# A hybrid decoder layer on one core: evacuations ordered behind dense products, inverses from blocks of 16, relayout transfers issued by SP

## The chip, the cores and the metric

The kernel runs on one core of a Trainium2 chip. The metric is the device time of one execution in microseconds (us). Engines: PE (TensorE) multiplies, DVE (VectorE), ACT (ScalarE) and POOL (GpSimd) work elementwise, SP (SyncE) issues most transfers; 16 DMA engines move data.

## The reference

The input is x of 1024 tokens x 1024 features, all float32, one layer:

```python
def swiglu(h, w1, w3, w2):
    return (jax.nn.silu(h @ w1) * (h @ w3)) @ w2
x = x + 0.5 * swiglu(rmsnorm(x, ffn1_norm), ...)          # D_FF = 2816
p = rmsnorm(x, mix_norm) @ w_in
y = concat(rwkv7_mixer(p[:D_SHIFT]), gmlp_mixer(pu, pv))  # 512 + 512 wide
x = x + y @ w_out
x = x + 0.5 * swiglu(rmsnorm(x, ffn2_norm), ...)
x = rmsnorm(x, final_norm)
```

The block above is condensed. The RWKV-7 mixer (8 heads of 64) is a recurrence over tokens, with a normalised key `kk = k*k_k / |k*k_k|`:

```python
sa = S @ a_t                      # a_t = -kk
S  = S * decay_t + sa b_t^T + v_t k_t^T   # b_t = kk * a
y_t = S @ r_t
```

The gMLP mixer multiplies by a causal 128 x 128 matrix inside chunks of 128 tokens.

## The kernel before, in words

**Dense products.** Every dense product is made of three products of 128x512 tiles in a reduced float32 format: each operand is split into a high part (ACT, a cast) and a low part (what the cast lost, a subtraction on DVE or POOL), and high x high, high x low and low x high are added up (`HI_LO`). `mm` (L192, instruction at L193) issues such a product, `rmm` (L201) a small one of the recurrence. The operands `wsp` (weights), `xt`, `xc` (activations) come from these splits.

**Stages.** FFN1 (to about 700 us), mixer (to about 1490), FFN2. Each FFN uses seven products p = 1..7 of half-size operands in place of eight. `down` (L478) runs p in the order 1, 5, 2, 3, 6, 7, 4; each p has 11 steps of 12 dense products. A step's `operands` (L483) loads weights and the hidden rows, forms differences on DVE (L493 to L497), casts on ACT (L500, L501) and makes low parts on DVE (L502) and POOL (L503). A finished bank is added to the residual by `add` (L519, instruction L521) on DVE: 12 additions after p = 1 and after p = 6, 8 after p = 7, 4 after each other one. `add` is given a high priority at the end and a place between products otherwise. In the last stage the final norm of row half 0 scales eight tiles (L716).

**Mixer.** w_in's columns come as weight pieces by `w_cols`, with the low part on POOL or DVE (L743). `pair` (L942) prepares decay, keys and values for two heads; it needs 1/|k|^2 per token and head, which `spread2` (L925, products `hm,sq`) and `back2` (L933, products `con,i`) sum and spread back. The recurrence runs in eight "octs" of 128 tokens (class `Oct`), each in chunks of 64. `prep` (L1120) forms SC, the products of keys with keys inside a chunk; `invert` (L1169) inverts 8x8 diagonal blocks on DVE, for which SC is written to DRAM (`ldr`, L1143), read back as blocks (`M`, L1172), the inverse written (`tdr`, L1187) and read back as `T` (L1191), all issued by ACT; `merge` (L1194) doubles the block size in three levels (8, 16, 32), each with products T,SC, then T,X and X,T; `chain` (L1226) carries the state S; `finish` (L1264) normalises the output (products `con,Y`). `w_out` (L766) multiplies by the output projection in two column halves, 192 products for each half of the tokens. `first_half` (L331) is FFN2's up product for one half of the tokens; it calls a `hook` into which the second `w_out` and then its statistics (products `one,xs`, `con,rr_r`) and `build`/`x_build` (`xc` tiles for the other half) are put.

**What sets the order.** The program is a set of Python tasks with a clock of their own (`Flow`): a task that says `yield 4.0` is resumed when 4.0 us of emitted work have passed, so these numbers set where its instructions stand among the others. A list scheduler then orders instructions by priority (`PR_RWKV`, `PR_CHAIN`, `PR_EVAC`) and by dependences. Each engine runs its instructions in that order.

Of the kernel before, what the change touches and what calls it, by code (L numbers as in the profile page):

```python
# [16 lines left out]
P = 128  # L17
# [28 lines left out]
CON = [("ident", 128), ("me", 128), ("m8", 32), ("m16", 32), ("m32", 32), ("bo", 128), ("cm", 256), ("tri", 128)]  # L46
# [7 lines left out]
def host_constants():  # L54
# [10 lines left out]
        **{f"m{b}": (s64 // (2 * b) == t32 // b) & (s64 // b % 2 == 1) for b in (8, 16, 32)},  # L65
# [82 lines left out]
class K:  # L148
    def __init__(self, ctx, tc, a, out):
# [12 lines left out]
        self.edge = None  # L162
# [28 lines left out]

    def mm(self, *args, **kw):  # L192
        i = self.nc.tensor.matmul(*args, **kw)  # L193
        if self.edge is not None:
# [75 lines left out]
    def apply(self, dst, res, gain, rb, out=None, ks=range(KT)):  # L270

        nc = self.nc
        for k in ks:
            t = self.xtp.tile([P, HALF], F32, name="silu", bufs=3)
            nc.vector.scalar_tensor_tensor(t, res[k // 2][:, k % 2], self.v(gain, k), rb, op0=ALU.mult, op1=ALU.mult)
# [202 lines left out]
    def down(self, pool, w2, res, done, loads):  # L478
# [40 lines left out]
        def add(p, bank, row, k):  # L519
            rv = res[row][k // 2][:, k % 2]  # L520
            ve.scalar_tensor_tensor(rv, bank, 0.5, rv, op0=ALU.mult, op1=ALU.add)  # L521
            done(p, row, k)

        for p, y, new, outs in plan:
# [18 lines left out]
            for o in outs:  # L543
                for f in range(4):
# [42 lines left out]
    def program(self):  # L587
# [39 lines left out]
        def task(row):  # L627
            yield 1.0
            rb = yield from self.spread(accs[row], "d" if row == 0 else "e", 2.5)
            if row == 0:  # L630
                rb = self.keep(rb)
                xm[0] = self.halves()
                for k in range(KT):
                    self.apply(xm[0], res[0], "gm", rb, ks=[k])
# [34 lines left out]
        yield ("rwkv", 0)  # L669
        accs = ([], [])  # L670
        out0 = yield from self.w_out(0, xres, accs[0], (self.mp, "h", 3))
# [6 lines left out]
        def hook(s):  # L678
            if state["done"] or not (("rwkv", 1) in flow.done or s >= 12):
# [4 lines left out]
        def second():  # L684
            yield ("rwkv", 1)
            crp.close()
            cm.close()
            p1, c1 = self.open("p1")
            yield from self.w_out(1, xres, accs[1], (p1,))
# [5 lines left out]
            rb1 = yield from self.spread(accs[1], "e")  # L695
            c1.close()
            cxq.close()
            flow.spawn(self.build(xres[1], "g2", w2, rbs2, stats2, ("xb", 1), True))
# [8 lines left out]
        def out(row):  # L707
# [5 lines left out]
            for k in range(KT):  # L713
                with self.hp(0 if row == 0 else PR_EVAC):
                    rv = res[row][k // 2][:, k % 2]
                    nc.vector.scalar_tensor_tensor(rv, rv, self.v("gf", k), rb, op0=ALU.mult, op1=ALU.mult)  # L716
# [35 lines left out]
    def w_cols(self, w, j, eng=None):  # L752
        return self.wtile([KT, P], w[j].rearrange("p (k n) -> p k n", k=KT), eng)
# [12 lines left out]
    def w_out(self, half, xres, acc, sums):  # L766
# [3 lines left out]
        for hf in range(2):  # L770
# [5 lines left out]
            for n, k in enumerate([4, 5, 6, 7, 0, 1, 2, 3]):  # L776
                raw = self.ws.tile([P, 2, HALF], F32, name="raw", bufs=RAWB)
# [19 lines left out]
    def mixer_consts(self):  # L797
# [20 lines left out]
        self.hm = mp.tile([P, 2], F32, name="hm")  # L818
        nc.scalar.copy(self.hm, self.c["bo"][:, 0::64])
        self.X = [mp.tile([P, NB, CH], F32, name=f"X{i}") for i in range(3)]  # L820
# [9 lines left out]
        nc.gpsimd.memset(self.S, 0.0)  # L830
        self.pcc = [mp.tile([P, PR, HALF // CH], F32, name=f"pcc{h}") for h in range(2)]
# [93 lines left out]
    def spread2(self, src):  # L925

        ps = self.psum("e")
        for t in range(4):
            self.rmm(ps[:, 2 * t:2 * t + 2], lhsT=src[:, t * P:(t + 1) * P], rhs=self.hm,
                     start=(t == 0), stop=True, skip_group_check=True)  # L930
        return ps[:, 0:8]

    def back2(self, small):  # L933
        ps = self.psum("e")
        for t in range(4):
            for h in range(2):
                self.rmm(ps[HS[h], t * P:(t + 1) * P],
                         lhsT=small[:, 2 * t + h:2 * t + h + 1].broadcast_to([P, CH]), rhs=self.c["ident"],
# [402 lines left out]
```

## Time and profile before

| | us |
|---|---|
| median of 3 runs | 2114.07 |
| lowest, highest | 2109.13, 2115.06 |
| profiled execution, its own time | 2114.52 |
| its span | 2112.4 |
| PE busy in it | 1971.0 (93%) |
| DVE, ACT, POOL busy | 1160.4 (55%), 700.5 (33%), 975.3 (46%) |
| mean granted PE clock | 0.962 of full |

Shares of busy time are means over stages. A matmul record of 128x512 in the timeline stands with its count (x132); in brackets stands the idle time of the engine before the group and what ended it. PEclk is the granted TensorE clock as a share of the full one (2.4 GHz; the lower level is 1.2 GHz).

### The profile page before, as it was taken

Reading aid. Unit: us, or ns where it says so; the run is one execution under the profiler, and the core shown is the slowest. Engines: PE = TensorE matmul, PEld = TensorE weight load, DVE = VectorE, ACT = ScalarE, POOL = GpSimd, SP = SyncE. Lnnn points to the kernel's source line nnn. Section 1 sums busy time; section 2 is a strip of 40 time slices with the busy share of each in tenths; the row PEclk is TensorE's granted clock in tenths of the full one; section 3 lists DMA queues with packets and bytes.
Section 4 is the critical chain, followed back from the end, with each engine's and each line's share of the span. In section 5 each row is a group of like instructions: output and inputs, shape, how many; then the busy total and the mean of one; then the engine's idle time right before and its main releaser. Section 6 shows DMA issues by size and latency. Waiting matters only on the chain. (4 is left out here: it accounts for less than half of the span.)

```text
span 2112.4 us, 34477 instructions
## 1 busy us (share of the span) xinstructions
PE 1971.0 (93%) x13408; PEld 1613.1 (76%) x13408; DVE 1160.4 (55%) x1645; ACT 700.5 (33%) x1205; POOL 975.3 (46%) x749
## 2 busy tenths in 40 slices
PE   6999999998998999999899898997899999999987
PEld 5787888887876778767788777876678888878866
DVE  6716666646658354445534344324756666655576
ACT  5433222223443443241312122233442222224432
POOL 3426665554555565353323133124455666545542
PEclk9999999999999999999999998998899999999998
DMA  8655444447644576553443455435654544476452
GB/s 284 237 165 170 169 159 160 159 149 275 195 151 139 194 242 212 130 203 106 149 132 98 118 157 177 118 126 188 212 175 162 170 168 159 136 264 193 141 178 101
DMA packets 235187, 360.34 MB, mean 171 GB/s; under 512 B 68240, under 2 KB 101008, under 8 KB 235024
## 3 DMA queue, kind: packets, MB, share of 16 engines
q1 hardware_dynamic: 181248, 342.43, 49.0%
q10 hardware_dynamic: 53776, 15.71, 3.2%
q8 instruction: 105, 1.72, 0.3%
q14 instruction: 58, 0.48, 0.1%
HBM read 260.53 MB, written 97.53 MB: 170 GB/s over the span
## 5 line engine op out<-in xcount | busy, mean ns | idle before, releaser
L193 PE MATMUL psd<-xt,wsp 128*128 128x512 f32 x1920 | 490.0, 412 | 12.4 <-ACT silu L352 3.9
L193 PEld LDWEIGHTS psd<-xt,wsp 128*128 128x128 f32 x1920 | 369.3, 196 | 107.2 <-DVE wsp L743 4.9
L743 POOL TENSOR_TENSOR wsp<-raw,wsp 128x512 fp32r<-128x512 f32 x170 | 228.9, 1367 | 363.2 <-ACT wsp L740 353.3
L193 PE MATMUL psd<-xc,wup 128*128 128x512 f32 x1584 | 374.8, 389 | 4.0 <-ACT wup L257 3.6
L193 PE MATMUL psd<-wsp 128*128 128x512 f32 x1440 | 342.6, 397 | 14.1 <-ACT wsp L501 9.5
L193 PEld LDWEIGHTS psd<-xc,wup 128*128 128x128 f32 x1584 | 297.0, 188 | 67.2 <-ACT wup L257 4.5
L193 PEld LDWEIGHTS psd<-wsp 128*128 128x128 f32 x1440 | 271.9, 191 | 77.1 <-ACT wsp L501 11.4
L503 POOL TENSOR_TENSOR wsp<-raw,wsp 128x512 fp32r<-128x512 f32 x154 | 230.1, 1498 | 215.6 <-ACT wsp L501 165.7
L193 PE MATMUL pse<-xc,wup 128*128 128x512 f32 x1056 | 254.4, 389 | 0.0
L258 POOL TENSOR_TENSOR wup<-wraw,wup 128x512 fp32r<-128x512 f32 x132 | 179.0, 1365 | 127.2 <-ACT wup L257 126.2
L193 PEld LDWEIGHTS pse<-xc,wup 128*128 128x128 f32 x1056 | 198.0, 188 | 41.5 <-ACT wup L257 0.5
L740 ACT CAST wsp<-raw 128x512 fp32r<-128x512 f32 x246 | 139.7, 617 | 150.1 <-PE psd L193 98.5
L502 DVE TENSOR_TENSOR wsp<-raw,wsp 128x512 fp32r<-128x512 f32 x110 | 104.9, 966 | 80.1 <-ACT wsp L500 79.9
L385 DVE TENSOR_TENSOR wt<-wraw 128x512 f32<-128x512 f32 x44 | 42.1, 958 | 183.1 <-DMA wraw<-in_ffn_w_dram 183.1
L257 ACT CAST wup<-wraw 128x512 fp32r<-128x512 f32 x132 | 81.3, 619 | 179.4 <-PE psd L193 109.7
L193 PE MATMUL pse<-wsp 128*128 128x512 f32 x396 | 110.1, 406 | 17.2 <-DVE wsp L502 12.7
L500 ACT CAST wsp<-raw 128x512 fp32r<-128x512 f32 x110 | 68.2, 620 | 165.8 <-PE psd L193 65.3
L193 PE MATMUL psc<-wsp 128*128 128x512 f32 x396 | 106.8, 399 | 0.0
L501 ACT CAST wsp<-raw 128x512 fp32r<-128x512 f32 x154 | 94.9, 617 | 32.4 <-DMA raw<-hd 25.7
L193 PEld LDWEIGHTS pse<-wsp 128*128 128x128 f32 x396 | 76.7, 196 | 36.7 <-DVE wsp L502 15.9
L743 DVE TENSOR_TENSOR wsp<-raw,wsp 128x512 fp32r<-128x512 f32 x76 | 60.4, 828 | 69.2 <-ACT wsp L740 56.5
L193 PEld LDWEIGHTS psc<-wsp 128*128 128x128 f32 x396 | 76.5, 194 | 16.4
(225 smaller groups left out, 2509.0 us busy)
## 6 DMA issues: line engine op xcount, KB each, us to landing
wraw<-in_ffn_w_dram SPq DMA_DIRECT2D x88, 512.0 KB, 4.6
raw<-hd SPq DMA_DIRECT2D x154, 256.0 KB, 3.5
raw<-in_ffn_w_dram SPq DMA_DIRECT2D x132, 256.0 KB, 3.2
raw<-in_ffn_w_dram SPq DMA_DIRECT2D x44, 512.0 KB, 4.3
raw<-in_w_in_dram SPq DMA_DIRECT2D x36, 512.0 KB, 4.1
hd<-u SPq DMA_DIRECT2D x66, 256.0 KB, 2.5
hd<-s SPq DMA_DIRECT2D x66, 256.0 KB, 5.0
sd<-silu SPq DMA_DIRECT2D x44, 256.0 KB, 3.4
```

The costliest lines, as they stand in the source:

```text
L193: i = self.nc.tensor.matmul(*args, **kw)
L257: nc.scalar.copy(t[:, 0], src)
L258: eng.tensor_tensor(t[:, 1], src, t[:, 0].bitcast(F32), op=ALU.subtract)
L385: ve.tensor_sub(t1, b12, b11)
L500: nc.scalar.copy(t[:, 0, 0], w)
L501: nc.scalar.copy(t[:, 0, 1], h)
L502: ve.tensor_tensor(t[:, 1, 0], w, t[:, 0, 0].bitcast(F32), op=ALU.subtract)
L503: ge.tensor_tensor(t[:, 1, 1], h, t[:, 0, 1].bitcast(F32), op=ALU.subtract)
L740: self.nc.scalar.copy(dst[:, 0, sl], src[:, sl])
L743: eng.tensor_tensor(dst[:, 1, sl], src[:, sl], dst[:, 0, sl].bitcast(F32), op=ALU.subtract)
```

## The change

Six parts. (1) `pace`: an order dependence without a semaphore that puts an instruction behind the last dense product emitted so far; used for `add` (except p = 4), the mixer's first activations and the final scalings of row half 0. The list of late additions goes f by f. (2) The inverse is made of 16x16 blocks on 64 partitions: two 8x8 inverses at a time and then the off-diagonal block by two multiplications and two reductions; `merge` has two levels. The waits of `invert` are 7.0, one 2.0 and 9.0. (3) ldr, M, tdr and T are issued by SP. (4) `spread2` and `back2` are gone: 16 one-column products per pair sum the squares, and 1/|k|^2 scales SC (four DVE operations of 128x128 per tile) and Bt (DVE in place of an ACT copy). (5) Low parts of `w_cols` alternate between DVE and POOL. (6) `w_out` waits for the recurrence only before its fifth of eight pieces; the hook for the second half waits for the last chain or s = 17; statistics and `build` behind it are a task of their own.

```diff
+    def pace(self, i):
+        self.tc.add_manual_dep(i.ins, self.last.name,
+                               mybir.DependencyInfo(mybir.DependencyClass.NoSync, mybir.DependencyReason.DATA),
+                               reason="order")
...
-            ve.scalar_tensor_tensor(rv, bank, 0.5, rv, op0=ALU.mult, op1=ALU.add)
+            i = ve.scalar_tensor_tensor(rv, bank, 0.5, rv, op0=ALU.mult, op1=ALU.add)
+            if p != 4:
+                self.pace(i)
...
-            for o in outs:
-                for f in range(4):
+            for f in range(4):
+                for o in outs:
...
-            if state["done"] or not (("rwkv", 1) in flow.done or s >= 12):
+            if state["done"] or not (("chain", 2 * NO - 1) in flow.done or s >= 17):
...
     def w_cols(self, w, j, eng=None):
+        if eng is None:
+            self.turns = 1 - self.turns
+            eng = self.nc.vector if self.turns else self.nc.gpsimd
...
             for n, k in enumerate([4, 5, 6, 7, 0, 1, 2, 3]):
+                if hf == 0 and n == 4:
+                    yield ("rwkv", half)
+                    sums = ready()
...
-        ss = self.spread2(sq)
+        ss = self.psum("e")
+        for i in range(HALF // CH):
+            for s in HS:
+                self.rmm(ss[s, i:i + 1], lhsT=sq[s, i * CH:(i + 1) * CH], rhs=self.one[s], start=(i == 0), stop=True,
+                         skip_group_check=True)
...
-        inv = self.back2(i8)
-        ve.tensor_mul(a, a, inv)
...
+                        nc.vector.scalar_tensor_tensor(d[:, p], m[:, p], inv[:, p, k:k + 1], c["me"],
+                                                       op0=ALU.mult, op1=ALU.mult)
...
-        nc.scalar.dma_start(M, self.diag(self.ldr))
+        nc.sync.dma_start(M, self.diag(self.ldr))
...
-        yield 4.0
+        yield 7.0
...
-            if t % 2:
-                yield 0.6
+            if t == 5:
+                yield 2.0
...
-                nc.scalar.dma_start(self.T[HS[h], n], self.matT(td[n], h))
-        yield 6.0
+                nc.sync.dma_start(self.T[HS[h], n], self.matT(td[n], h))
+        yield 9.0
...
-        for lvl, bs in enumerate((8, 16, 32)):
+        for lvl, bs in enumerate((16, 32)):
```

DVE at the change from p = 1 to p = 5 in FFN1's down product, before. L493 forms differences, L502 low parts, L521 the additions (`rd` and `res` are the residual's tiles, `psd` the banks):

```order
L493 TENSOR_TENSOR dt<-raw,dt 128x512
L502 TENSOR_TENSOR wsp<-dt,wsp 128x512
L521 SCALAR_TENSOR_TENSOR rd<-psd,rd 128x512 x4
L521 SCALAR_TENSOR_TENSOR res<-psd,res 128x512 x8
L493 TENSOR_TENSOR dt<-raw,dt 128x512 x4
L502 TENSOR_TENSOR wsp<-dt,wsp 128x512 x2
```

The same place of the changed program, where L504, L513 and L532 are the lines of the same three operations:

```order
L504 TENSOR_TENSOR dt<-raw,dt 128x512 x2
L513 TENSOR_TENSOR wsp<-dt,wsp 128x512
L532 SCALAR_TENSOR_TENSOR rd<-psd,rd 128x512
L532 SCALAR_TENSOR_TENSOR res<-psd,res 128x512 x2
L532 SCALAR_TENSOR_TENSOR rd<-psd,rd 128x512
L504 TENSOR_TENSOR dt<-raw,dt 128x512
L513 TENSOR_TENSOR wsp<-dt,wsp 128x512
L504 TENSOR_TENSOR dt<-raw,dt 128x512 x2
L532 SCALAR_TENSOR_TENSOR res<-psd,res 128x512 x2
```

The twelve additions stood in one block and now stand a few at a time among differences and low parts.

PE at the end of the recurrence and the second `w_out` (the 192 products `psd<-wsp`), before; `psd<-xt,wsp` are dense products of FFN2's first half, `psd<-xc,wup` the first that need x_build's tiles:

```order
L202 MATMUL psc<-WA,Bt 64x64 x8
L193 MATMUL psd<-xt,wsp 128x512 x12
L202 MATMUL psc<-WA,SC 64x64 x8
L202 MATMUL pse<-con,Y 64x64 x16
L193 MATMUL psd<-wsp 128x512 x192
L202 MATMUL pse<-one,xs 128x1 x8
L202 MATMUL pse<-con,rr_r 128x128 x4
L193 MATMUL psd<-xt,wsp 128x512 x216
L193 MATMUL psd<-xc,wup 128x512 x2
```

And now:

```order
L210 MATMUL psc<-WA,SC 64x64 x8
L200 MATMUL psd<-xt,wsp 128x512 x51
L210 MATMUL pse<-con,Y 64x64 x16
L200 MATMUL psd<-xt,wsp 128x512 x24
L200 MATMUL psd<-wsp 128x512 x10
L200 MATMUL psd<-xt,wsp 128x512 x12
L200 MATMUL psd<-wsp 128x512 x182
L200 MATMUL psd<-xt,wsp 128x512 x30
L210 MATMUL pse<-one,xs 128x1 x8
L200 MATMUL psd<-xt,wsp 128x512 x9
L210 MATMUL pse<-con,rr_r 128x128 x4
L200 MATMUL psd<-xt,wsp 128x512 x129
```

Fifty-one dense products of the first half moved ahead of con,Y and 39 between the end of w_out and the statistics' last step; 168 are left between w_out's end and the first product on `xc`, where 216 were. In the whole program dense and small products on PE change over 206 times, before 234 times.

SP in the changed program, in the mixer's first octs; the names with x and o are the recurrence's own stores and loads through DRAM, `raw` a weight piece:

```order
L1159 DMA ldr<-SC 64x8x64 x2
L1126 DMA oG<-xG_138 128x4x128
L1193 DMA M<-ldr 64x16x16
L1126 DMA oB<-xB_135 128x4x128
L766 DMA raw<-in_w_in_dram 128x1024
L1126 DMA oK<-xK_136 128x4x128
L1126 DMA oV<-xV_137 128x4x128
L1223 DMA tdr_0_5532<-D 64x16x16
L1223 DMA tdr_1_5534<-D 64x16x16
L1227 DMA T<-tdr_0_5532 64x8x64 x2
L1227 DMA T<-tdr_1_5534 64x8x64 x2
```

The four kinds of relayout transfer stood on ACT before and now stand between SP's loads of weights and of the recurrence's operands.

## Rows read from the trace of the kernel before

**Rows 1.** Table of windows: start:end; length, busy (instructions) per engine, PEclk, DMA, GB/s.

```profile
core 0: us, PE busy (x) PEld busy (x) DVE busy (x) ACT busy (x) POOL busy (x), PEclk, DMA share, GB/s
...
490.00:530.00 40.00, 35.47 (x145) 28.43 (x144) 31.05 (x38) 14.66 (x27) 19.16 (x14) 0.91 0.67 224
620.00:700.00 80.00, 67.54 (x289) 52.83 (x287) 67.02 (x84) 32.02 (x53) 41.21 (x35) 0.96 0.49 164
830.00:1330.00 500.00, 457.04 (x6008) 380.61 (x6007) 224.02 (x445) 134.84 (x244) 162.97 (x152) 0.93 0.48 139
1420.00:1440.00 20.00, 11.57 (x95) 9.14 (x95) 6.57 (x12) 4.29 (x8) 6.44 (x5) 0.74 0.17 55
1483.00:1500.00 17.00, 11.39 (x46) 9.81 (x45) 9.10 (x14) 4.48 (x7) 3.56 (x3) 0.70 0.78 265
...
1890.00:1926.00 36.00, 31.48 (x130) 24.87 (x129) 28.60 (x36) 13.53 (x24) 18.45 (x13) 0.95 0.57 182
2016.00:2062.00 46.00, 38.20 (x160) 30.56 (x159) 37.07 (x45) 15.25 (x25) 17.58 (x13) 0.89 0.52 178
```

**Rows 2.** PE's timeline, both down products: start, length, line, tiles, count [idle before].

```profile
500.26 1.22 PE L193 MATMUL pse<-wsp 128*128 128x512 f32 x2 [4.53 <-ACT wsp L500]
...
671.47 2.07 PE L193 MATMUL psd<-wsp 128*128 128x512 f32 x4 [7.03 <-ACT wsp L501]
...
1926.66 30.08 PE L193 MATMUL psd<-wsp 128*128 128x512 f32 x132
...
2049.71 1.22 PE L193 MATMUL pse<-wsp 128*128 128x512 f32 x2 [4.64 <-DVE wsp L502]
```

**Rows 3.** DVE's timeline just before two of these waits.

```profile
494.09 4.87 DVE L521 SCALAR_TENSOR_TENSOR res<-psd,res 128x512 f32<-128x512 f32 x8
...
2039.57 9.48 DVE L716 SCALAR_TENSOR_TENSOR rd<-rd,vec,rbk 128x512 f32<-128x512 f32 x8 [3.35 <-ACT rbk L283]
```

**Rows 4.** PE's timeline in the mixer: small products that go, and what follows.

```profile
757.36 0.95 PE L202 MATMUL pse<-hm,sq 128*128 128x2 f32 x8
...
764.88 1.09 PE L202 MATMUL pse<-con,i 128*64 128x128 f32 x16
...
870.60 1.12 PE L202 MATMUL pse<-T,SC 64*64 64x32 f32 x32
871.66 5.16 PE L193 MATMUL psd<-xt,wsp 128*128 128x512 f32 x21
```

**Rows 5.** PE's timeline: a dense run between small products.

```profile
1168.15 4.69 PE L193 MATMUL psd<-xt,wsp 128*128 128x512 f32 x19
```

**Rows 6.** DVE: scaling of SC (timeline); low parts of weights (page's groups).

```profile
840.37 1.29 DVE L1137 TENSOR_TENSOR SC<-pse,con 128x512 f32<-128x512 f32 x2 [3.96 <-PE pse L202]
...
L743 DVE TENSOR_TENSOR wsp<-raw,wsp 128x512 fp32r<-128x512 f32 x76 | 60.4, 828 | 69.2 <-ACT wsp L740 56.5
```

**Rows 7.** PE's timeline from the recurrence's last output to the second w_out's statistics.

```profile
1433.34 1.98 PE L202 MATMUL pse<-con,Y 64*64 64x64 f32 x32 [8.43 <-POOL Y L1278]
...
1484.68 0.61 PE L193 MATMUL psd<-wsp 128*128 128x512 f32 x2
1489.56 3.58 PE L202 MATMUL pse<-one,xs 128*128 128x1 f32 x16 [4.27 <-DVE xs L233]
```

**Rows 8.** DVE's timeline: the last xc tile of x_build.

```profile
1534.43 0.68 DVE L263 TENSOR_TENSOR xc<-nx,xc 128x512 fp32r<-128x512 f32 x1
```

**Rows 9.** ACT's timeline: the first oct's relayouts, and a copy behind another's.

```profile
836.44 1.36 ACTq L1143 DMA_DIRECT2D ldr<-SC  x2
841.03 0.38 ACTq L1172 DMA_DIRECT2D M<-ldr  x1
...
847.66 2.10 ACTq L1187 DMA_DIRECT2D tdr<-D  x2
...
852.63 0.60 ACTq L1191 DMA_DIRECT2D T<-tdr  x1
...
1194.84 0.58 ACT L1158 COPY Bt<-pse 128x512 f32<-128x512 f32 x1 [13.61 <-DMA T<-tdr]
```

More of the change, by code (lines that the diff above doesn't have):

```diff
@@ L161, in __init__ @@
         self.ws = e(tc.tile_pool(name="ws", bufs=1, reuse_waits="tile"))
-        self.edge = None
+        self.edge = self.last = None
+        self.turns = 0
         base = self.base
@@ L268, in halves, with apply @@
         return [self.xtp.tile([P, 2, 2, HALF], F32R, name="xt", bufs=4) for _ in range(4)]
-    def apply(self, dst, res, gain, rb, out=None, ks=range(KT)):
+    def apply(self, dst, res, gain, rb, out=None, ks=range(KT), pace=False):
         nc = self.nc
@@ L668, in program @@
         yield from self.gmlp(1, xm[1])
-        yield ("rwkv", 0)
         accs = ([], [])
-        out0 = yield from self.w_out(0, xres, accs[0], (self.mp, "h", 3))
+        out0 = yield from self.w_out(0, xres, accs[0], lambda: (self.mp, "h", 3))
         rb = yield from self.spread(accs[0], "e")
@@ L682, in hook, with opened, second, last_build @@
             return second()
-        def second():
-            yield ("rwkv", 1)
+        def opened():
             crp.close()
             cm.close()
-            p1, c1 = self.open("p1")
-            yield from self.w_out(1, xres, accs[1], (p1,))
+            p1, state["close"] = self.open("p1")
+            return (p1,)
+        def second():
+            yield from self.w_out(1, xres, accs[1], opened)
+            flow.spawn(last_build())
+        def last_build():
+            rb1 = yield from self.spread(accs[1], "e")
+            state["close"].close()
+            cxq.close()
             def stats2(pool):
@@ L693, in stats2 @@
                 rbs2.append(self.keep(rb1, pool))
[L695 to L698, printed above, removed]
+            yield from self.build(xres[1], "g2", w2, rbs2, stats2, ("xb", 1), True)
         yield from self.first_half(x12, w2, hook)
@@ L764, in dense_T, with w_out @@
         return o
-    def w_out(self, half, xres, acc, sums):
+    def w_out(self, half, xres, acc, ready):
         nc = self.nc
@@ L817, in mixer_consts @@
         self.omk = lambda i: vc[:, 26 + i:27 + i]
-        self.hm = mp.tile([P, 2], F32, name="hm")
-        nc.scalar.copy(self.hm, self.c["bo"][:, 0::64])
-        self.X = [mp.tile([P, NB, CH], F32, name=f"X{i}") for i in range(3)]
+        self.X = [mp.tile([P, NB, CH], F32, name=f"X{i}") for i in range(2)]
         for x in self.X:
@@ L830, in mixer_consts @@
         nc.gpsimd.memset(self.S, 0.0)
+        self.inv = [mp.tile([P, PR, HALF // CH], F32, name=f"inv{h}") for h in range(2)]
         self.pcc = [mp.tile([P, PR, HALF // CH], F32, name=f"pcc{h}") for h in range(2)]
@@ L921, in wrap @@
             yield y
[L925 to L938, printed above, removed]
-                         start=True, stop=True)
-        return ps
     def pair(self, half, p, k, v, r):
@@ L1126, in prep @@
         yield 2.5
+        inv = K_.inv[self.half]
         SC = self.SC = self.tl("SC", 2, (P, 2, NC, PR, 2, CH))
@@ L1148, in prep, with turned @@
         yield 0.5
-    def turned(self, name, X):
+    def turned(self, name, X, scale=None):
         K_ = self.K
@@ L1212, in merge @@
             pt = K_.psum("e", (P, 2, NB, CH // 2))
-            for n in range(1 if lvl == 2 else 2):
+            for n in range(1 if lvl == 1 else 2):
                 for b in range(NB):
@@ L1219, in merge @@
                             K_.rmm(pt[s, 1, b], lhsT=T[s, 0, b], rhs=one(X[s, b], 0), start=True, stop=True)
-            for n in range(1 if lvl == 2 else 2):
+            for n in range(1 if lvl == 1 else 2):
                 d = part(T[:, n], 1 - n)
```

67 lines of the change are left out of this document (46 added, 21 removed).

## The prediction

> **What bounds the kernel now.** I read the busy shares first: TensorE (PE) has the most. So the question is where PE waits, and where its clock is granted low after a wait. The table of windows says how much each stretch loses [rows 1]: a window's length less PE's busy time is idle, and the length times what PEclk lacks to 1.00 is what the lower of the two clocks (1.2 instead of 2.4 GHz) costs. 490:530 loses 4.5 + 3.6 us, 620:700 12.5 + 3.2, the long mixer window 43.0 + 35.0, 1420:1440 8.4 + 5.2, 1483:1500 5.6 + 5.1, 1890:1926 4.5 + 1.8 and 2016:2062 7.8 + 5.1. PE's timeline then names the waits. In the two down products they are for operands that ACT and DVE still have to split [rows 2], and DVE's timeline shows why: just before, it ran evacuations or the final norm in one block, 4.87 us for eight additions and 9.48 us for eight scalings [rows 3]. One dense product takes 30.08/132 = 0.228 us [rows 2].
>
> The sum is made against the profiled execution, span 2112.4 us, 2114.5 us by its own time, 0.4 us above the median of the runs shown.
>
> **a. Work taken from PE, -28 us.** One merge level of three goes in each of the eight octs: three blocks of 32 small products (T,SC, then T,X and X,T), 24 blocks of 1.06 us, start to start [rows 4], 25.4 us. `back2` goes: eight blocks of 1.09 us, 8.7 us; `spread2`: eight of 0.95 us, 7.6 us [rows 4]. Added are eight groups of 16 one-column products, which the trace doesn't show; as eight-row and 32-row blocks both take about 1 us, I put each at 0.9 (bounds 0.5 and 1.1), 7 us. Each break in a dense run costs something too: 19 products took 4.69 us, 0.36 more than 19 x 0.228 [rows 5]; the new order has 14 fewer such breaks, 5 us. Together -25.4 - 8.7 - 7.6 + 7 - 5 = -40. Some of it lies where PE waits for the recurrence anyway (PE is busy 91% of the long window, and small products crowd around its waits), so I count 0.7 of it; bounds -22 and -40. DVE pays for it beside PE: per oct four more operations like the 0.65 us one [rows 6] and finer scalings, some 4 us; it is busy 224 of 500 us there, so nothing.
>
> **b. Additions of FFN1's down product ordered behind dense products, -10 us.** The two windows lose 23.8 us. The adds now stand one or two at a time between splits, as the order shows; the same DVE work remains. At 620:700 DVE is busy 67.0 of 80 us [rows 1], so spreading alone cannot remove every wait. I take a little under half; bounds 0 and -21.
>
> **c. The same in FFN2's down product, and the final scalings of row 0, -8 us.** 6.3 + 12.9 = 19.2 us are lost there. The 9.48 us block [rows 3] goes, which the 4.64 us wait [rows 2] follows. Again a little under half; bounds 0 and -17.
>
> **d. The tail of the recurrence before the second w_out, -12 us.** PE waits 8.43 us for Y and then runs slowly [rows 1, 7]: 13.6 us. In the new order 51 dense products stand ahead of that instruction, 11.6 us of work, more than the wait; 12 of 13.6 is taken, for the hook comes from a different place in the first half. Bounds -5 and -13.6.
>
> **e. The statistics after the second w_out, -4 us.** They cost 10.7 us now [rows 1], the 4.27 us wait for xs among it [rows 7]. Afterwards dense products of the first half stand between these steps, so I count all of it as gained. But then a new wait comes: the first products on `xc` stand 168 dense products (38.3 us) and some 4 us of small ones behind w_out's end at 1485.3, while DVE made the last `xc` at 1535.1 [rows 7, 8], 49.8 us after it. So PE is there 7 us too early. Net -4; bounds -10.7 and +3.
>
> **f. The waits of the mixer, -12 us.** 78 us are lost in the long window. The chain that must pass through DRAM is plain in ACT's timeline [rows 9]: ldr out at 836.4, M back from 841.0, tdr out at 847.7, T back from 852.6. ACT stands in this chain and its copies queue behind it, once 13.61 us. With the issues on SP, ACT's copies and splits no longer stand behind them. The emission waits, 7 and 9 instead of 4 and 6, put products with operands of this chain later. Most of PE's waits there are short and have other causes (loads of B, DVE's SC and WA), so a sixth of the loss; bounds -45 and +10.
>
> The remaining edits go at nothing. 36 low parts more on DVE (0.83 us each [rows 6]) are 30 us in stretches in which DVE has slack, and POOL is freed from as many; if that cover failed, a weight piece would be late by at most its own 0.8 us. w_out(0) starting before the recurrence's end only exchanges which products fill the same gap: bounds -5 and +5.
>
> The sum: -28 - 10 - 8 - 12 - 4 - 12 = -74, so 2114.5 - 74 = 2040.5, and 2040 against the median.
>
> The Trainium skill ("DMA: Bandwidth & Descriptors", section "Issuing engines are not separate DMA queues") says that DMAs issued by different engines end up on the same 16 DMA engines, and that another issuer saves only the time of the issuing. By that rule term f would be zero for the move, since the same bytes move on engines busy 48% of the long window [rows 1]. The row with 13.61 us shows ACT kept in order by something other than bandwidth, which the rule does not speak of; that is the second rival.
>
> **The rivals.**
> Relayouts on SP hold the weights back (**slower**). SP issues nearly all loads. From ldr's issue to T's the chain takes 852.6 - 836.4 = 16.2 us [rows 9], in which SP would stand at waits while weight loads queue behind. Cover: four raw buffers, three ahead, 24 products each: 3 x 24 x 0.228 = 16.4 us, just enough. Against it: the new order puts loads between the steps. Without f the other terms give -62; it decides from 62/8 = 7.8 us exposed per oct. All of 16.2 x 8 = 130 exposed gives 2114.5 - 62 + 130 = 2182.
>
> The moved issues and longer waits bring nothing, and less of the removed work lay on the path: a at -22, f at +2: 2114.5 - 22 - 10 - 8 - 12 - 4 + 2 = 2060. For it: recurrence steps follow one another, so what leaves one wait shows up in the next.
>
> DVE is the limit in the down products: the adds are spread but their waits come back in smaller pieces, b and c zero, 2058. For it: 67.0 of 80 us busy.
>
> The waits go nearly all: a -36, b -20, c -17, d -13.6, e -10, f -30 give -127, 1988. For it: the low clock after each wait goes with the wait.
>
> **How the numbers follow.** My forecast has 0.50 (about 2020 to 2060 by itself), the second rival 0.20, the third 0.10, nearly all waits 0.15, SP 0.05. The range 1995 to 2085 takes in the forecast and the second and third rivals with both their shortfalls added (2078), and leaves out SP and half of the fast case. A measurement here tells about 0.3% (6.3 us) from no change. Only the SP rival ends above that, 0.05; of the others some 0.03 end within it, if the second and third meet and d and e fail too; faster has 0.92.
>
> **What would show it right or wrong.** On DVE the additions stand singly among splits, and the waits of 4.53, 7.03 and 4.64 us before a phase's first product shrink under 2 us (b, c). PE's groups T,SC and T,X lose a third of their rows (a). No wait of 8 us stands before con,Y (d). A wait of about 7 us stands before the first product on xc after the second w_out (e). ACT no longer waits for tdr, SP does (f). If waits of PE or ACT for raw<-in_w_in appear in the mixer, SP has become the limit and I am wrong on the other side; if the long window loses over 80 us again, f is wrong.

## The result, and the profile after

The changed kernel takes 2081.24 us (median of 4 runs, 2078.73 to 2085.79) against 2112.66 us for the kernel before in the same runs: a ratio of 0.9853, 95% interval 0.9828 to 0.9877. That is 31 us less where 74 were forecast; the time lies in the range (1995 to 2085), at its upper end. The profiled execution took 2082.39 us, with a span of 2080.6 us.

To see where the time went I cut each trace at the same two places, the end of the mixer's first statistics and the first product on `xc`, and split PE's time between them into idle, "low clock" (half of the time at the lower clock in which PE was busy) and the rest, which is its work at full clock:

| us | before: length, idle, low clock, work | after |
|---|---|---|
| FFN1 | 717.1: 42.8, 10.2, 664.0 | 715.1: 42.9, 14.8, 657.5 |
| mixer | 840.9: 70.4, 42.2, 728.3 | 814.2: 82.5, 48.8, 682.9 |
| FFN2 | 554.4: 28.2, 9.0, 517.2 | 551.3: 24.5, 8.7, 518.1 |

Low clock is read off steps of some 3.4 us in the trace, so it is good to a few us in a stage. Each such row comes from one profiled execution. The two FFNs gave 5 us. In the mixer 45 us of work are gone, more than the 40 of term a before its factor of 0.7, but idle and low clock together ("the waits" from here on) went from 112.6 to 131.3 us, where terms d, e and f wanted 28 us less.

The table of windows for the places of [rows 1] at their new times, the mixer first (columns as there):

```profile
715.12:1529.29 814.17, 731.70 (x7510) 602.62 (x7508) 426.63 (x758) 258.21 (x456) 275.83 (x232) 0.93 0.53 163
815.00:1315.00 500.00, 433.50 (x5354) 364.43 (x5353) 258.45 (x515) 129.65 (x233) 141.89 (x131) 0.90 0.49 144
...
485.00:525.00 40.00, 37.34 (x155) 29.57 (x154) 32.79 (x39) 16.31 (x29) 22.18 (x15) 0.96 0.71 241
618.00:698.00 80.00, 67.81 (x278) 52.60 (x277) 62.64 (x82) 30.72 (x50) 39.22 (x33) 0.94 0.46 154
1405.00:1425.00 20.00, 20.00 (x121) 16.37 (x117) 7.46 (x13) 8.20 (x15) 6.48 (x5) 1.00 0.40 139
1467.00:1485.00 18.00, 18.00 (x91) 15.21 (x90) 7.68 (x11) 5.74 (x10) 6.24 (x6) 1.00 0.89 300
1862.00:1898.00 36.00, 35.17 (x150) 27.37 (x149) 34.05 (x38) 15.91 (x28) 23.26 (x15) 1.00 0.65 206
1988.00:2034.00 46.00, 41.24 (x179) 33.62 (x178) 37.62 (x47) 16.21 (x28) 20.70 (x14) 0.93 0.47 159
```

The long window, now 815:1315, is 66.5 us idle where it was 43.0. PE is busy without a break, at full clock, where it stood before con,Y and the second w_out's statistics (1405:1425, 1467:1485). FFN1's second window lost as much as before: 12.2 us idle and 4.8 of clock, for 12.5 and 3.2. PE's timeline at the places of [rows 2, 7]:

```profile
670.93 7.35 PE L200 MATMUL psd<-wsp 128*128 128x512 f32 x24 [5.33 <-ACT wsp L512]
...
1416.90 1.15 PE L210 MATMUL pse<-con,Y 64*64 64x64 f32 x32
...
1480.70 1.84 PE L210 MATMUL pse<-one,xs 128*128 128x1 f32 x16
...
1529.29 0.73 PE L200 MATMUL psd<-xc,wup 128*128 128x512 f32 x2 [2.09 <-ACT wup L265]
...
2029.18 22.70 PE L200 MATMUL psd<-wsp 128*128 128x512 f32 x91 [3.16 <-DVE wsp L513]
```

The last con,Y and one,xs have no wait. The wait of 7.03 us ahead of FFN1's p = 4 is still 5.33. DVE's timeline just before that wait, in the kernel before:

```profile
664.73 2.47 DVE L521 SCALAR_TENSOR_TENSOR res<-pse,res 128x512 f32<-128x512 f32 x4
667.12 2.47 DVE L521 SCALAR_TENSOR_TENSOR res<-psc,res 128x512 f32<-128x512 f32 x4
669.51 0.68 DVE L497 TENSOR_TENSOR raw<-raw,dt 128x512 f32<-128x512 f32 x1
```

And after the change, with the additions one or two at a time, as the order had them:

```profile
662.80 0.68 DVE L532 SCALAR_TENSOR_TENSOR res<-pse,res 128x512 f32<-128x512 f32 x1
663.40 1.84 DVE L283 SCALAR_TENSOR_TENSOR silu<-rd,vec,rbk 128x512 f32<-128x512 f32 x2
665.17 1.28 DVE L532 SCALAR_TENSOR_TENSOR res<-pse,res 128x512 f32<-128x512 f32 x2
666.37 1.42 DVE L271 TENSOR_TENSOR xt<-silu,xt 128x512 fp32r<-128x512 f32 x1
667.71 0.74 DVE L283 SCALAR_TENSOR_TENSOR silu<-rd,vec,rbk 128x512 f32<-128x512 f32 x1
668.38 0.68 DVE L532 SCALAR_TENSOR_TENSOR res<-pse,res 128x512 f32<-128x512 f32 x1
668.98 0.67 DVE L508 TENSOR_TENSOR raw<-raw,dt 128x512 f32<-128x512 f32 x1
```

DVE has no gap there. The difference that p = 4 needs (L497, now L508) comes at 668.98, where it came at 669.51: other operations of DVE stand among the additions and take the place that the block left.

PE's waits in the mixer after the change (what waited <- for what: us in total, times, longest):

```profile
PE pse L210 <- issue: 9.0, 2, 5.7
PE pse L210 <- DMA AR<-xR: 8.7, 3, 3.5
PE psc L210 <- DVE S L1291: 6.8, 2, 3.5
PE pse L210 <- DVE h L241: 5.7, 1, 5.7
PE pse L210 <- DVE X L1244: 5.5, 2, 4.5
```

("issue" is time in which the profile shows nothing that PE waited for.) There is no long one; they are many and spread over the recurrence. For AR<-xR it was 3.7 us before. ACT waits for tdr no longer; SP's waits at the four relayout transfers add up to 92 us.

### The profile page after: what moved, and what is told of

Its sections match the earlier page's. It is cut to its first block, busy times and chain, and to the rows that moved or that the text cites. A ratio compares the mean times of both kernels' runs of the same rounds, so it can differ in the third digit from the quotient of the medians.

```text
span 2080.6 us, 33103 instructions
## 1 busy us (share of the span) xinstructions
PE 1930.7 (93%) x12704; PEld 1584.4 (76%) x12704; DVE 1223.5 (59%) x1737; ACT 697.0 (33%) x1196; POOL 939.0 (45%) x712
## 5 line engine op out<-in xcount | busy, mean ns | idle before, releaser
L200 PE MATMUL psd<-xt,wsp 128*128 128x512 f32 x1920 | 483.4, 410 | 18.0 <-ACT silu L363 5.2
L200 PEld LDWEIGHTS psd<-wsp 128*128 128x128 f32 x1440 | 270.3, 189 | 80.0 <-ACT wsp L512 10.2
L514 POOL TENSOR_TENSOR wsp<-raw,wsp 128x512 fp32r<-128x512 f32 x154 | 230.2, 1502 | 203.9 <-ACT wsp L512 172.5
L762 POOL TENSOR_TENSOR wsp<-raw,wsp 128x512 fp32r<-128x512 f32 x134 | 186.1, 1407 | 295.7 <-ACT wsp L759 275.6
L266 POOL TENSOR_TENSOR wup<-wraw,wup 128x512 fp32r<-128x512 f32 x132 | 177.0, 1349 | 128.9 <-ACT wup L265 127.2
L513 DVE TENSOR_TENSOR wsp<-raw,wsp 128x512 fp32r<-128x512 f32 x110 | 110.6, 1016 | 66.7 <-ACT wsp L511 66.4
L762 DVE TENSOR_TENSOR wsp<-raw,wsp 128x512 fp32r<-128x512 f32 x112 | 93.2, 864 | 84.0 <-ACT wsp L759 74.1
L512 ACT CAST wsp<-raw 128x512 fp32r<-128x512 f32 x154 | 94.9, 617 | 21.3 <-DMA raw<-hd 16.6
```

Source lines behind the costliest of these rows:

```text
L266: eng.tensor_tensor(t[:, 1], src, t[:, 0].bitcast(F32), op=ALU.subtract)
L512: nc.scalar.copy(t[:, 0, 1], h)
L513: ve.tensor_tensor(t[:, 1, 0], w, t[:, 0, 0].bitcast(F32), op=ALU.subtract)
L514: ge.tensor_tensor(t[:, 1, 1], h, t[:, 0, 1].bitcast(F32), op=ALU.subtract)
L762: eng.tensor_tensor(dst[:, 1, sl], src[:, sl], dst[:, 0, sl].bitcast(F32), op=ALU.subtract)
```

## The experiments

The three theories at the start: the relayouts on **SP** hold the loads of AR and oB back; **DVE** is loaded too much by the change; **latency**, that is, the recurrence's steps wait for one another wherever PE has less to do. A ratio is to the kernel before, measured on the same chip (0.9853 for the whole change); waits are idle plus low clock of the mixer, from each kernel's profiled execution. Executions of one kernel differ by up to 22 us in some of these kernels (2083 to 2105 for f1_inv), so the profile tells the structure, and the ratios the time.

**e1_act: relayouts back on ACT.**

```diff
-                    nc.sync.dma_start(self.matT(self.ldr, h),
+                    nc.scalar.dma_start(self.matT(self.ldr, h),
...
```

> The changed kernel (2081 us) with its 72 relayout transfers (ldr, M, tdr, T) issued by ACT again, nothing else. Theory SP: SP now stands some 90 us at the waits of these transfers, and the loads of AR and oB behind them come late (PE's waits for AR<-xR rose from 3.7 to 8.7 us, 9.0 us more have no releaser). Then the kernel gets faster by 8 to 18 us, 2063 to 2073, and AR waits fall back under 4 us. Theory latency (the recurrence's steps now wait for one another where PE had small products before): the issuer does not matter, 2076 to 2086. Theory ACT (the move paid, and something else took it back): 2087 to 2100, with ACT's copies waiting for tdr again.

Ratio 0.9823 (0.9803 to 0.9843), waits 123.7. Hardly faster than the change, and the two intervals overlap; waits for AR<-xR 6.5 us. SP isn't the main cause.

**e2_pool: low parts back on POOL.**

```diff
-            eng = self.nc.vector if self.turns else self.nc.gpsimd
+            eng = self.nc.gpsimd
```

> The changed kernel with the low parts of weight columns on POOL again where no engine was named (36 pieces of 128x512 go back from DVE). Theory DVE: DVE works 417 us in the mixer instead of 372, and PE's waits for DVE's S, X, D, SC, oG (some 27 us) come from it; 30 us less DVE work gives 5 to 15 us, 2066 to 2076. Theory latency: those waits are for a step whose input is late, DVE itself is free, so 2077 to 2087. If POOL was the limit for these pieces before: 2088 or more.

0.9797 (0.9760 to 0.9833), waits 121.3: faster by half a per cent, as the DVE theory has it, though the two intervals still touch, with 10 us less waiting. I had put this edit at nothing. The profile doesn't single it out: each of the four undoings e1 to e4 has less waiting than the change (121.3 to 128.9 us for 131.3).

**e3_wait: the old emission waits.**

```diff
-        yield 7.0
+        yield 4.0
...
-            if t == 5:
-                yield 2.0
+            if t % 2:
+                yield 0.6
...
-        yield 9.0
+        yield 6.0
```

> The changed kernel with the old emission waits in invert (4.0, then 0.6 after every second step, then 6.0; 12.4 us for 18.0). Theory latency: later emission keeps PE from standing at D and T, so with the old waits PE waits some 1 to 3 us more per oct: 2089 to 2105. Theory fill (the longer waits put the recurrence's steps later, so that they meet where little dense work is left): 2065 to 2075. Neither: 2076 to 2086.

0.9784 (0.9757 to 0.9812), some 14 us faster than the change: the longer waits cost time here, and the two intervals are apart. One wait of another kind came in, on PE's timeline:

```profile
1519.61 1.22 PE L200 MATMUL psd<-xc,wup 128*128 128x512 f32 x2 [15.60 <-ACT wup L265]
```

That is the wait of term e. In this order 144 dense products stand between w_out's end and the first on `xc`, not 168 (2.09 us of wait). In both the first product on `xc` comes at about the same distance from w_out's end, 56.3 us here and 55.2 in the change, so x_build sets it.

**e4_pace: no order dependence.**

```diff
     def pace(self, i):
-        self.tc.add_manual_dep(i.ins, self.last.name,
-                               mybir.DependencyInfo(mybir.DependencyClass.NoSync, mybir.DependencyReason.DATA),
-                               reason="order")
+        return
```

> The changed kernel without the order dependence of additions, activations and final scalings (the list of late additions stays f by f). By the profile of the changed kernel the two FFN ends are 3.4 and 3.1 us shorter than before; if that is what the order gives, 2084 to 2092, with waits of 4 to 5 us back ahead of p = 5 in FFN1 and of 4 us in FFN2's p = 7. If the first FFN2 products or the mixer gained from it too (activations of row 0): 2092 to 2105. If nothing hangs on it: 2078 to 2083.

0.9830 (0.9810 to 0.9850): nothing in the time hangs on it, although there are waits again where the kernel before had them, three on PE's timeline:

```profile
498.26 2.07 PE L198 MATMUL pse<-wsp 128*128 128x512 f32 x4 [4.53 <-ACT wsp L509]
...
668.06 0.79 PE L198 MATMUL psd<-wsp 128*128 128x512 f32 x1 [4.53 <-ACT wsp L509]
...
1871.89 0.94 PE L198 MATMUL pse<-wsp 128*128 128x512 f32 x2 [4.83 <-DVE wsp L511]
```

The first was 4.53 us before and 1.51 in the changed kernel, the second 7.03 and 5.33; the third stands in FFN2's p = 5, where the kernel before had one of 3.55 and the changed kernel none over 0.40. Without the dependence FFN1 is 2.6 us shorter and FFN2 1.1 us longer than with it. That is less than the same stage differs from profile to profile: over the ten profiled kernels with the dependence FFN1 takes 712.0 to 718.7 us, over the ten without 712.5 to 719.3. FFN2 takes 548.9 to 555.2 us with it and 552.4 to 559.4 without (means 550.8 and 556.4).

**c1_wait_pool: the edits of e2_pool and e3_wait together**, of which the first line is

```diff
-        yield 7.0
+        yield 4.0
...
```

> The changed kernel with the old emission waits and with the low parts back on POOL, the two undoings that gained most so far (about 13 and 10 us, each against 2083.6 us for the changed kernel on this scale, 0.9853 of 2114.7). Theory parts: each edit costs the mixer its own waits, so the gains add: 2055 to 2064. Theory scatter: any other order of the same work meets about as many waits, the changed kernel's order was an unlucky one, so no adding up: 2066 to 2078.

0.9777 (0.9747 to 0.9807), waits 115.1, with 17.24 us ahead of the first `xc` product. No clear addition: it is as fast as e3_wait alone.

**c3_246: only the inverses, the norm path and w_out's place**: the edits of e1_act to e4_pace, and

```diff
-            for f in range(4):
-                for o in outs:
+            for o in outs:
+                for f in range(4):
```

> Only the inverses from 16x16 blocks, the new norm path and w_out's new place; ACT issues the relayouts, old waits, low parts on POOL, additions without the order dependence and in the old sequence. Theory parts: 2083.6 - 7 - 10 - 13 - 5 = 2045 to 2056. Theory scatter: 2064 to 2078.

0.9814 (0.9782 to 0.9845), waits 122.8. The parts do not add up.

**c4_24: only the inverses and the norm path**: c3_246 with w_out, hook and second as in the kernel before, so

```diff
             for n, k in enumerate([4, 5, 6, 7, 0, 1, 2, 3]):
-                if hf == 0 and n == 4:
-                    yield ("rwkv", half)
-                    sums = ready()
...
```

> Only the inverses from 16x16 blocks and the new norm path, w_out as before. This measures the work taken from PE alone (term a, -28 with bounds -22 and -40): 2075 to 2093 if it lies on the path as I counted it, the long window's idle time staying near 43 us. Theory latency: what leaves PE comes back as waits of the recurrence, 2095 to 2110.

0.9895 (0.9856 to 0.9935), 22 us for 43 us of work removed (728.3 to 685.2). The time lies at the upper edge of where the work alone puts it, but the waits rose from 112.6 to 128.3, so a third of what was taken came back.

**e5_out: the whole change without w_out's new place.**

```diff
+        yield ("rwkv", 0)
         accs = ([], [])
-        out0 = yield from self.w_out(0, xres, accs[0], lambda: (self.mp, "h", 3))
+        out0 = yield from self.w_out(0, xres, accs[0], (self.mp, "h", 3))
...
-            if state["done"] or not (("chain", 2 * NO - 1) in flow.done or s >= 17):
+            if state["done"] or not (("rwkv", 1) in flow.done or s >= 12):
...
```

> The changed kernel with w_out, its hook and the statistics behind it as before (the wait for the recurrence ahead of w_out, the hook at s = 12, x_build in the same task). Terms d and e (-12 and -4) and w_out(0) are undone: 2093 to 2104 if they hold, with a wait of about 8 us ahead of the last con,Y and one of about 4 us for xs. If this part brought nothing, or its gain is paid for in w_out(0): 2078 to 2088.

0.9830 (0.9804 to 0.9856): not slower. con,Y and one,xs wait again (15.7 and 4.3 us in all), but the products of the scores (AR with oB and oK) wait 18.0 us for 34.2 in the changed kernel. So d and e happened where I said, and the time was lost elsewhere. Without the rest of the change the same part does gain: c3_246 differs from c4_24 by it alone and is 0.8% (17 us) faster, with the intervals apart.

**d1_double: the removed level's products added again, as doubles.**

```diff
             for b, (i, p) in enumerate(cp):
                 for s in HS:
-                    K_.rmm(px[s, b], lhsT=SC[s, 0, i, p, 0], rhs=one(T[s, 1, b], 0), start=True, stop=True)
+                    for _ in range(2 - lvl):
+                        K_.rmm(px[s, b], lhsT=SC[s, 0, i, p, 0], rhs=one(T[s, 1, b], 0), start=True, stop=True)
...
```

> The changed kernel with the three blocks of 32 small products of merge's first level computed twice, into the same place: 96 rows per oct, 24.7 us more of PE work in all, exactly what the dropped level had. Theory latency (the removed work had filled waits, so that it came back as waiting): the doubles fall into waits and cost 0 to 10 us, 2081 to 2091. Theory work (every product removed was worth its time, and the waits grew for another reason): 20 to 30 us, 2101 to 2112.

1.0075 (1.0060 to 1.0090): 46 us slower than the change, for 19 us more work; the waits rose to 160.6, 19.9 of them for AR<-xR. That is against the latency theory (work put back does not fill waits), and against the work theory too. But the order moved elsewhere as well: 17.7 us stand ahead of the first `xc` product, with 144 dense products of cover, where the change had 2.09, and that is over half of the 29 us more waiting. What the doubles cost on their own path isn't told apart from that.

**b1_sp, b2_wait, b3_small: single edits on the kernel before.** b1_sp moves the four relayouts to SP, b2_wait takes the longer waits (both as above, the other way round), b3_small has

```diff
-        yield 6.0
+        yield 6.4
```

> The kernel before with its relayout transfers on SP, nothing else. Idle plus clock loss of the mixer was 112.6 us before and 115 to 131 in all eight kernels with the new inverses. Theory scatter (the order before was a lucky or well-tuned one; any other order of the recurrence waits 5 to 15 us more): 2115 to 2130, waits 118 to 128. Theory latency (the waits grew because work was removed): the waits stay at 108 to 117, 2108 to 2119. My term f (the move helps): 2095 to 2108.

> The kernel before with the longer emission waits in invert (7.0, 2.0 after the fifth step, 9.0). Theory scatter: 2115 to 2130 and waits of 118 to 128 us in the mixer. Theory latency: 2108 to 2120. My term f: 2095 to 2108. If longer waits are bad by themselves, as in the changed kernel (13 us): 2122 to 2130.

> The kernel before with one emission wait 0.4 us longer (6.0 to 6.4 at the end of invert), which changes the order of some 500 rows on PE and nothing else. Theory scatter: any such change moves the time by 5 us or more, up more likely than down (2117 to 2130). Theory latency: it does nothing, 2109 to 2117.

0.9965 (0.9951 to 0.9980), 1.0008 (0.9991 to 1.0025) and 0.9972 (0.9954 to 0.9989), waits 96.1, 105.0 and 104.8. The order before was not a lucky one; with the move to SP the kernel is 7 us faster, the longer waits do nothing there, and a wait changed by 0.4 us moves the time by 6 us: that is how far an order alone goes, so the 7 us can't be put down to the move. All four kernels with the old inverses and norm path have less waiting than any of the ten with both new ones so far (115 to 161), which points at these two. It is a hint and no more: in four of the ten (e3_wait, c1_wait_pool, c3_246, d1_double) 15.6 to 17.7 us of it is the wait for `xc`, which w_out's new place brings.

**f1_inv and f2_norm: each of the two alone, on the kernel before.** f1_inv is c4_24 with `spread2`, `back2`, `a*inv`, the mask by one operation and ACT's copy of Bt put back; f2_norm is the kernel before with

```diff
-        ss = self.spread2(sq)
+        ss = self.psum("e")
+        for i in range(HALF // CH):
+            for s in HS:
+                self.rmm(ss[s, i:i + 1], lhsT=sq[s, i * CH:(i + 1) * CH], rhs=self.one[s], start=(i == 0), stop=True,
+                         skip_group_check=True)
...
-        inv = self.back2(i8)
-        ve.tensor_mul(a, a, inv)
...
+                        nc.vector.scalar_tensor_tensor(d[:, p], m[:, p], inv[:, p, k:k + 1], c["me"],
+                                                       op0=ALU.mult, op1=ALU.mult)
```

> The kernel before with the inverses from 16x16 blocks and two merge levels alone (ACT issues, old waits, old norm path). PE loses 25 us of work. Theory inverse (the longer inverse on DVE, about 6.9 for 4.1 us, and the earlier merge put the waits of about 10 to 15 us into the mixer that all kernels with both edits show): 2098 to 2105, waits (idle plus clock) 115 to 125. Theory norm (the waits come from the finer scaling of SC and from Bt on DVE): 2084 to 2092, waits 105 to 112.

> The kernel before with the new norm path alone: one-column products, 1/|k|^2 applied in SC and Bt on DVE; 8x8 blocks and three levels as before. PE loses some 18 us of work. Theory norm: 2103 to 2112, waits 117 to 130. Theory inverse: 2090 to 2098, waits 105 to 113.

f1_inv: 0.9906 (0.9873 to 0.9939), work 728.3 to 702.0, waits 111.5, as before. **f2_norm: 1.0098 (1.0068 to 1.0127), 21 us slower, though its work is 15 us less (713.3): the waits are 139.6.** On the kernel before, the norm path takes products from PE and makes PE wait for more than they took. Next to the new inverses it only breaks even: c4_24 is f1_inv with the norm path, has 17 us less work and 17 us more waiting, and takes the same time within the two intervals (0.9895 and 0.9906).

What such a wait can look like, on PE's timeline of f2_norm and on DVE's (`con,oB`, `con,oK` and `con,oV` turn an operand by a product with the identity):

```profile
855.83 0.86 PE L193 MATMUL psd<-wsp,xt 128*128 128x256 f32 x5
860.12 0.91 PE L202 MATMUL pse<-con,oK 64*64 64x64 f32 x22 [3.42 <-DVE SC L1124]
862.13 1.43 PE L202 MATMUL pse<-con,oV 64*64 64x64 f32 x21 [1.10 <-DVE Bt L1154]
```

```profile
851.63 1.13 DVE L1128 SCALAR_TENSOR_TENSOR SC<-pse,inv,con 128x128 f32<-128x128 f32 x4 [0.89 <-PE pse L202]
852.67 0.68 DVE L1124 TENSOR_TENSOR SC<-pse,con 128x512 f32<-128x512 f32 x1
858.73 0.16 DVE L1176 TENSOR_TENSOR Dtmp<-D,M 128x1 f32<-128x1 f32 x1 [5.38 <-DMA M<-ldr]
...
859.38 0.68 DVE L1124 TENSOR_TENSOR SC<-pse,con 128x512 f32<-128x512 f32 x1
```

DVE stands 5.38 us at the inverse's first step, since M isn't back; behind it in DVE's order is the mask of the last score tile, which holds one of the two `pse` banks, so that con,oK, which needs a bank, keeps PE idle 3.42 us. This shows how DVE's order can hold a bank; it doesn't show that the new path made the wait. DVE's waits for M add up to 24.5 us before and 26.6 in f2_norm, and to 31.7 in h2_best, the fastest kernel below.

Where the waits grew can be read from pairs of kernels with and without the norm path. PE's idle time in the mixer before `pse` products that DVE released is 36.3 us in f2_norm against 29.2 before, 39.3 in c4_24 against 25.9 in f1_inv, 31.7 in the change against 20.7 in h1_oldnorm, 30.5 in g12_hook against 10.7 in h2_best (the last two pairs follow below). The part before prep's own products (the scores of AR with oB and oK, and the three that turn) is 26.9 us in f2_norm for 13.6 before, and that growth is as large as the whole mixer's (83.2 us idle for 70.4). In all seven profiled kernels with the old norm path these take 10.4 to 27.4 us (median 14.8; the 27.4 is b2_wait, so order alone can do it too), in the thirteen with the new one 21.9 to 44.5 (median 26.7). DVE's work grew little: it is busy 396.3 us of f2_norm's mixer for 380.0 before, 2 us per oct.

**x2_bt: f2_norm with Bt from ACT.** The kernel leaves out Bt's factor 1/|k|^2.

```diff
-            K_.nc.vector.tensor_mul(v(t), v(ps), w)
+            K_.nc.scalar.activation(t, ps, AF.Identity, scale=1e-5)
```

> The new norm path alone on the kernel before (1.0098 of it, 139.6 us of waits), with Bt taken out of its bank by ACT with a constant factor, as it was copied before, in place of DVE's multiplication with 1/|k|^2: the factor 1/|k|^2 of Bt is left out. If Bt on DVE (8 operations of 0.68 us, behind whatever DVE has queued, with the bank held meanwhile) brings the waits: 1.000 or less, waits under 122. If the scaling of SC in four operations, ahead of the relayouts, brings them (M lands later, PE waited 12.3 us for the inverse): 1.006 to 1.012, waits over 130.

1.0089 (1.0056 to 1.0123), waits 131.7: Bt on DVE isn't it, or some 8 us of the waits. Left are the scaling of SC in four operations (1.13 us where the mask took 0.65 [rows 6]) and the one-column products. No run separates these two. The traces point to the scaling: the idle time grew before prep's products (23.2 us here), among which it stands, while before the one-column products PE is idle 1.7 us in f2_norm and not at all here.

**h1_oldnorm: the whole change without the norm path** (the same pieces put back as in f1_inv).

> The whole change without the new norm path: spread2, back2 and a*inv as before, SC masked by one DVE operation per tile, Bt copied by ACT. PE gets some 17 us of work back. Theory norm (this path alone brings 16 to 27 us of waits, as in the kernel that has nothing else, where they rose from 112.6 to 139.6): the waits of the mixer fall from 131 to between 104 and 115, time 2070 to 2084 against 2083.6 (on the scale of 2114.7): the path is worth nothing or less than nothing. Theory mixture (the waits depend on the sum of all orders, not on this path): waits stay over 122, 2092 to 2102.

0.9806 (0.9755 to 0.9857), median 2064.61 us; the interval still touches that of the change, so within the change the path's cost in time isn't clear of noise. In the profiles the waits of the mixer fall from 131.3 to 91.7 us, for 19.7 us more work. From the table of windows, the mixer of h1_oldnorm:

```profile
714.36:1508.72 794.36, 725.34 (x7445) 594.64 (x7444) 411.13 (x709) 261.42 (x464) 275.10 (x233) 0.96 0.54 167
```

**g12_hook and h2_best: towards a faster kernel.** g12_hook is c1_wait_pool with the hook back at s = 12; h2_best is g12_hook without the norm path.

```diff
-            if state["done"] or not (("chain", 2 * NO - 1) in flow.done or s >= 17):
+            if state["done"] or not (("chain", 2 * NO - 1) in flow.done or s >= 12):
```

> The fastest kernel so far (old waits, low parts on POOL, 0.978 of before) with the second w_out's hook at s = 12 again. In that kernel 144 dense products stood between w_out's end and the first on xc, and PE waited 15.6 us there; now 216 do, as in the kernel before. Theory cover (term e: that wait is x_build's time less these products): the wait goes, 2046 to 2056 against 2112.6. If w_out, placed earlier, waits for the recurrence instead: 2060 to 2070.

> The fastest order so far (old emission waits, low parts on POOL, hook at s = 12; 0.980 of before) without the new norm path. If that path is worth less than nothing everywhere: 0.970 to 0.977, waits of the mixer under 95 for 106.8. If its waits were already hidden in that order, only its work counts (17 us more): 0.983 to 0.989.

g12_hook: 0.9802 (0.9761 to 0.9844), no gain on c1_wait_pool (0.9777) in the time. The wait of 17.24 us for `xc` is gone (1.79), as cover says, with 216 products; but w_out's products, now earlier, wait 10.9 us for 2.4. Its waits (106.8 us) lie under the 112.6 of the kernel before although it has the norm path; but they come from an execution of 2058.18 us, where the other three took 2071.72 to 2074.04. **h2_best: 0.9679 (0.9632 to 0.9726), median 2040.32 us, faster than both kernels;** the norm path alone is 1.2% between these two, with the intervals apart. Its mixer, from the table of windows:

```profile
718.72:1489.80 771.08, 723.81 (x7446) 589.02 (x7444) 406.15 (x682) 262.51 (x464) 311.25 (x264) 0.97 0.55 172
```

47.3 us idle and 21.3 of low clock, for 82.5 and 48.8 in the change.

## Why the prediction was right or wrong

The direction was right, the size not: 31 us of 74. Two steps failed, and with them the adding up.

The first is in term a, the sentence by which DVE "pays for it beside PE" and "so nothing": I priced the finer scalings by DVE's mean share of the long window [rows 1]. The work was even less than I said (2 us per oct, not 4), and still that path cost 21 us in f2_norm and 1.2% between h2_best and g12_hook. It cost nothing between f1_inv and c4_24, and within the whole change 39.6 us of waits for 19.7 us of work in one pair of profiles, in the time not clear of noise (h1_oldnorm). That the norm path does this is shown; that it does so through what stands behind the scalings in DVE's order and the two `pse` banks is argued from one place and from where the waits grew.

The second is in term f: the longer emission waits, forecast as part of -12, cost 14 us (e3_wait), the largest clear loss that one undoing in the change shows.

- **a.** The work was sized well: 45.4 us gone for 40. For the inverses the factor of 0.7 held about (26.3 us of work, 20 us of time in f1_inv); for the norm path it gave from nothing to a loss.
- **b and c.** -10 and -8 forecast, 2.0 and 3.1 us in the profile, and nothing by e4_pace. For b this is the third rival, to which I gave 0.10: DVE had no gap just ahead of p = 4, and the spread additions leave the operand it waits for where it was, 0.53 us sooner. For c the lengths of FFN2 over twenty profiles allow 1 to 6 us, which the time of e4_pace doesn't confirm.
- **d and e.** At their places right: the idle time is gone. The forecast counted 13.6 and 10.7 us of loss there, but took the lower clock over the whole window, also where PE stood; counted while PE worked, it is 10.5 and 9.6 (and 29.4 for 35.0 of clock in the long window). The new wait came with 2.09 us where I said 7. The rule behind e, that x_build sets when the first product on `xc` can start, is borne out: it comes 55.2 to 57.1 us after w_out's end in the eight kernels with 168 or 144 products between, where I had reckoned with 49.8. The wait was short in the change since 7.1 us of other waits stand among the 168. In the whole change the sum gained nothing by d and e (e5_out is as fast); between c4_24 and c3_246 the same part gave 17 us, as forecast.
- **f.** -12 forecast. The sign against it came: by its own count the long window loses 66.5 + 50 us where it lost 43 + 35. With the move to SP the kernel before gets 7 us faster, about as much as a change of order alone can do (b3_small), and in the change the move shows nothing clear; the longer waits do nothing there and cost 14 us here. The second rival was right that the move and the longer waits bring nothing; its 2060 was still too low, since it had no part that adds waits. With the norm path out, the mixer's waits do fall, by 21 us (h1_oldnorm), near the 28 of d, e and f together.
- **The remaining edits.** Low parts on DVE were put at nothing; undoing them gave about half a per cent in the change (e2_pool) and nothing clear on top of the old waits (c1_wait_pool).
- **SP as the bound** (0.05) did not come, though SP stands 92 us at the relayouts: in h1_oldnorm and h2_best they are on SP as well.

I had reckoned with waits that stay, not with an edit that removes work from the busiest engine and is slower by itself. That the time fell inside the range is luck in part: its upper end came from the shortfalls of the second and third rivals, and much of the gain was lost to something else. Open: which half of the norm path does it, why it costs 21 us on one kernel and nothing on another, and why low clock takes so large a share (26 of the 39.6 us, 14 of the 27.0 in f2_norm).

## What to carry to other kernels

Work taken from the bound engine must be weighed with what replaces it on another engine: here 2 us more per oct on DVE went with a kernel that was 21 us slower. What share of the time that engine is busy didn't tell it; which banks or buffers stand behind the replacement in its order is the thing to look at, though that this is the mechanism wasn't proven here. When a package of edits gains less than the sum, put each edit alone on the old kernel; of the four measured so (inverses, norm path, move to SP, emission waits) one was slower alone, and leaving it out of the package (with the emission waits, the low parts and the hook as before) more than doubled the gain. An edit that gains on one kernel can gain nothing on another: w_out's new place gave 17 us and nothing, the norm path nothing and -21. A long wait that vanishes at its place is no gain until the stage is shorter: compare the length of whole stages between the same two instructions.

## What the runs showed of the hardware that was not expected

The lower clock costs from a third to three fifths as much as the idle time. In the mixer, the trace has 15 stretches at the lower clock before, 18 after the change and 9 in h1_oldnorm and h2_best, at a cost of 42.2, 48.8, 22.7 and 21.3 us, beside 70.4, 82.5, 69.0 and 47.3 us of idle time; idle fell by only 13.5 us from the change to h1_oldnorm, low clock by 26.1. And executions of one and the same kernel lie up to 1% apart here (2083.2 to 2104.9 us in f1_inv, 2058.2 to 2074.0 in g12_hook), so four executions each did not settle a difference of half a per cent between two such kernels (e2_pool, h1_oldnorm).
